# First product of a block inverse with 64 columns of the inverse as stationary operand, and the first loads of the recurrence on another queue

## Chip, cores, metric

The kernel runs on one core of a Trainium2 chip. The metric is device microseconds for one execution of the whole program. Engines are named as the profile names them: PE is TensorE (PEld its weight loads), DVE is VectorE, ACT is ScalarE, POOL is GpSimd, SP is SyncE, which here only issues DMAs; ACT can issue DMAs too (ACTq).

## What is computed

A one-layer encoder: layer norm, one input projection, a Fourier mixer and a bidirectional gated DeltaNet side by side, an output projection, layer norm, a squared-ReLU MLP, layer norm. 2048 tokens and 16 meta tokens, width 1024, 4 heads of 128. The part that matters is the DeltaNet in chunked form:

```
l_mat = einsum("rbhncd,rbhnsd->rbhncs", k_beta, k) * decay_strict
unit_lower = l_mat + eye(CHUNK)
rhs = concatenate([v_beta, k_beta * exp(g_cum)[..., None]], axis=-1)
sol = triangular_solve(unit_lower, rhs, left_side=True, lower=True, unit_diagonal=True)
...
def step(S, inp):
    v_new = val - kcd @ S
    o = qd @ S + attn @ v_new
    S = S * chunk_decay + kt.T @ v_new
```

The kernel works in chunks of 128 tokens (16 steps, two directions, 4 heads) and does not solve: it forms the inverse of the unit triangular 128x128 matrix of each head and multiplies by it.

## The kernel before

The program runs in stages: norm and Fourier transform, the q/k/v projection with its convolution, the projection of z and the gates (`phase_zg`, about 514 to 981 us), the recurrence (`phase_delta`, about 980 to 1233 us), merge and output projection, MLP. A scheduler lays out each engine's instructions; an engine then runs its own list in order.

**Side work.** While PE runs the projection of z and the gates (three f16 matmuls, L95 to L97, per product, PSUM tiles `mm`, added up by DVE at L652), `phase_zg` pops pieces from a generator, `Delta.prep`, two per pop. Each `yield` in that generator ends a piece. `prep` builds per chunk and direction the strictly triangular matrix `N` (L1095) and the attention matrix `A`, stores both to DRAM, cuts the 32x32 diagonal blocks out of `N` (`diag`, with a sign change on ACT, L1112), inverts these blocks on DVE (`invert_blocks`, L997/L999, tiles `ivq`, `ivt`), and lastly runs `solve` for step 0 of both directions.

**solve** puts the 128x128 inverse of one step and direction together from its four inverted 32x32 diagonal blocks, loaded as `ad`. `X` holds the inverse, `XT` its transpose; all these tiles carry the name `hb` in the profile, since they lie in the memory of former `hb` tiles. It is a chain of four products per head, each in f32, with `yield`s between:

- P1 (L1175, PSUM 128x64): stationary `N` (128 columns), moving 64 columns of `XT`; only two 32x32 blocks of the result are wanted. ACT copies them with a minus sign to `V` (L1177).
- P2 (L1181): stationary `V` (64 columns), moving 64 columns of `X`: the 32x32 blocks beside the diagonal. DVE transposes one into `XT` (L1182) and copies two into `X` (L1184).
- P3 (L1188): stationary 64 columns of `N`, moving `XT`; ACT copies it with a minus sign to `W` (L1189).
- P4 (L1193): stationary `W`, moving `X`: the 64x64 block, copied to `X` by DVE (L1194).

Before P1 the blocks `ad` are spread into `X` and `XT`, transposed by DVE (L1169) and as they are by ACT (L1170).

**step** (L1258 to L1303) is one step of the recurrence in one direction: `S` times k (L1258, then DVE makes `vt`, L1260), `S` times q (L1266, ACT makes `qs`, L1269), the inverse times `vt` (L1275, ACT makes `vn`, L1278), the state update (L1283, DVE L1289) and the output (L1295, DVE L1301). Its PSUM tiles are `psc`, those of `solve` `psh` in the recurrence and `psg` before it. In direction 1 the first step has no state, and its L1258, L1266 are absent.

**phase_delta** interleaves by hand, with `go`, the two directions' step s and the two `solve`s of step s+1. In step 0 the loads of `vt` and `ktk` were issued from ACT (`q = nc.scalar if step == 0`), as was that of `ad` for step 1; all other loads of the recurrence (`N`, `A`, `kq`: 256, 256 and 512 KB a step and direction; `vt`, `ktk`: 256 KB each; `ad`: 64 KB) go from SP, two steps ahead. ACT also issues the stores `gz` of the last groups of `phase_zg` (L930).

Of the kernel before, what the change touches and what calls it, by code (L numbers as in the profile page):

```python
# [18 lines left out]
P = 128  # L19
# [3 lines left out]
NT = 16  # L23
# [3 lines left out]
HD = 4  # L27
# [980 lines left out]
class Delta:  # L1008
    RING = 5

    def __init__(self, k, pr):
        self.k = k
        self.d1 = [k.dram.tile([P, 32, 32], F32, name="d1_%d" % b) for b in range(4)]
        self.d2 = [k.dram.tile([P, 32, 32], F32, name="d2_%d" % b) for b in range(4)]
        self.dm1 = k.dram.tile([HD, 16, 16], F32, name="dm1")
        self.dm2 = k.dram.tile([HD, 16, 16], F32, name="dm2")
        self.NAd = {(q, d): k.dram.tile([2, P, HD, P], F32, name="na_%d_%d" % (q, d))
                    for q in range(NT) for d in range(2)}
        self.o1 = {}
        self.N, self.A, self.kq = {}, {}, {}  # L1020

        t = [half_block(pr).rearrange("p a b c -> p (a b c)").bitcast(F32) for _ in range(4)]
        self.uq = [t[3][:, 1024 * d:1024 * d + 1024].rearrange("p (h e c) -> p h e c", h=HD, e=2) for d in range(2)]
        t = [u[:, 512 * j:512 * j + 512].rearrange("p (h c) -> p h c", h=HD) for u in t for j in range(4)]
        self.S = [k.kp.tile([P, HD, P], F32, name="Sm"), None]
        self.X = [t[0:2], t[2:4]]
        self.XT = t[4:6]
        self.V, self.W = [[u[:, :, 64 * d:64 * d + 64] for d in range(2)] for u in t[6:8]]
        self.Nf, self.Af = t[8:10], t[10:12]
        self.t = t  # L1030
        for t in self.X[0] + self.X[1] + self.XT + self.V + self.W:
            k.nc.gpsimd.memset(t, 0.0)
        self.nx = 0

    def open_prep(self, ctx):
        k, nc = self.k, self.k.nc
        self.sp = ctx.enter_context(k.pool("dsa"))
        self.pg = ctx.enter_context(k.pool("dpg", bufs=3, space=PSUM))
        self.mneg = self.sp.tile([P, 2, P], BF16, name="mneg")
# [37 lines left out]
    def stage2(self, n):  # L1077

        k, nc, sp = self.k, self.k.nc, self.sp
        E = []  # L1080
        kq = self.load_kq(n, sp, 2)
        for d in range(2):
            E.append((yield from self.decay(n + 1, d, P)))
        NA = [[sp.tile([P, HD, P], F32, name="%s%d" % (a, d), bufs=1) for a in "NA"] for d in range(2)]
        for j in range(2):
            yield
            ps = self.pg.tile([P, HD, P], F32, name="psg").rearrange("p (a b) c -> p a b c", b=2)
            for e in range(2):
                h = 2 * j + e
                nc.tensor.matmul(ps[:, e], lhsT=kq[:, h, 0], rhs=kq[:, h], start=True, stop=True)  # L1090
            hh = slice(2 * j, 2 * j + 2)
            for d in range(2):
                for e in range(2):
                    h = 2 * j + e
                    nc.vector.scalar_tensor_tensor(  # L1095
                        out=NA[d][0][:, h], in0=ps[:, e, 0], scalar=k.beta[:, n + 1, 4 * d + h:4 * d + h + 1],
                        in1=E[d][:, h], op0=ALU.mult, op1=ALU.mult)
                nc.vector.tensor_tensor(out=NA[d][1][:, hh], in0=ps[:, :, 1], in1=E[d][:, hh], op=ALU.mult)
        for d in range(2):
            st = self.chunk(n, d)  # L1100
            self.diag(NA[d][0], st, d)
            for a in range(2):
                nc.sync.dma_start(out=self.NAd[st, d][a], in_=NA[d][a])
        yield

    def diag(self, N, step, d):

        k, nc, sp = self.k, self.k.nc, self.sp
        nd = sp.tile([P, HD, 32], F32, name="nd", bufs=2)
        for b in range(4):  # L1110
            s = slice(32 * b, 32 * b + 32)
            nc.scalar.activation(out=nd[s], in_=N[s, :, s], func=AF.Copy, scale=-1.0)  # L1112
# [21 lines left out]
    def prep(self):  # L1134

        yield from self.stage2(0)
        yield from self.stage2(NT - 1)
        yield from self.meta()
        for half, bts in ((range(1, 4), (0, 3)), (range(4, 8), (1, 2))):
            for q in half:  # L1140
                yield from self.stage2(q)
                yield from self.stage2(NT - 1 - q)
            for b in bts:
                yield from invert_blocks(self.k, self.sp, self.d1[b], self.d2[b], 32, P)
                yield
        for d in range(2):
            self.N[0, d], self.A[0, d] = self.t[8 + d], self.t[10 + d]
            for a, u in enumerate((self.N, self.A)):
                self.k.nc.sync.dma_start(out=u[0, d], in_=self.NAd[0, d][a])
            self.kq[0, d] = self.uq[d]  # L1150
            self.k.nc.sync.dma_start(out=self.kq[0, d], in_=self.k.kqd[self.chunk(0, d)])
            yield
            yield from self.solve(0, d, self.sp, self.pg, "psg")

    def solve(self, step, d, sp, pp, pname):

        k, nc = self.k, self.k.nc
        N = self.N[step, d]
        ad = sp.tile([P, HD, 32], F32, name="ad", bufs=2)
        o = ((step % 4) * 2 + d) * 16  # L1160
        (nc.scalar if step == 1 else nc.sync).dma_start(out=ad, in_=self.d2[step // 4][o:o + 16].rearrange("(h b) r j -> (b r) h j", b=4))
        X, XT, V, W = self.X[d][step % 2], self.XT[d], self.V[d], self.W[d]
        blk = lambda b: slice(32 * b, 32 * b + 32)
        half = lambda a: slice(64 * a, 64 * a + 64)
        f, s = ((0, 1), (1, 0))[d]
        pair = lambda a, z: blk(2 * a + z)
        x, xt = (XT, X) if d == 0 else (X, XT)
        for b in range(4):
            nc.vector.transpose(xt[blk(b), :, blk(b)], ad[blk(b)])  # L1169
            nc.scalar.copy(x[blk(b), :, blk(b)], ad[blk(b)])  # L1170
        yield
        cols = lambda t, h, z: t[:, h].rearrange("p (a z c) -> p a z c", z=2, c=32)[:, :, z]
        ps = pp.tile([P, HD, P], F32, name=pname)
        for h in range(HD):
            nc.tensor.matmul(ps[:, h, :64], lhsT=N[:, h], rhs=cols(XT, h, f), start=True, stop=True)  # L1175
        for a in range(2):
            nc.scalar.activation(out=V[pair(a, s), :, blk(a)], in_=ps[pair(a, s), :, blk(a)], func=AF.Copy, scale=-1.0)  # L1177
        yield
        ps = pp.tile([P, HD, P], F32, name=pname)
        for h in range(HD):  # L1180
            nc.tensor.matmul(ps[:64, h, :64], lhsT=V[:, h], rhs=cols(X, h, s), start=True, stop=True)  # L1181
        nc.vector.transpose(XT[pair(f, s), :, pair(f, f)], ps[blk(f), :, blk(f)])  # L1182
        for a in range(2):
            nc.vector.tensor_copy(X[pair(a, f), :, pair(a, s)], ps[blk(a), :, blk(a)])  # L1184
        yield
        ps = pp.tile([P, HD, P], F32, name=pname)
        for h in range(HD):
            nc.tensor.matmul(ps[:64, h, :64], lhsT=N[:, h, half(s)], rhs=XT[:, h, half(f)], start=True, stop=True)  # L1188
        nc.scalar.activation(out=W[half(s)], in_=ps[:64, :, :64], func=AF.Copy, scale=-1.0)  # L1189
        yield  # L1190
        ps = pp.tile([P, HD, P], F32, name=pname)
        for h in range(HD):
# [44 lines left out]
    def step(self, step, d):  # L1237
# [99 lines left out]
def phase_delta(k, dl):  # L1337
    with ExitStack() as cd:
# [4 lines left out]
        def loads(upto):  # L1343
            while dl.loaded <= min(upto, NT - 1):
                for d in range(2):
                    dl.load(dl.loaded, d)
                dl.loaded += 1

        for s in range(NT):
            st = [dl.step(s, d) for d in range(2)]  # L1350
            if s == 0:
                for g in st:
                    next(g)
                loads(1)
            ho = [dl.solve(s + 1, d, dl.cp, dl.ph, "psh") for d in range(2)] if s < NT - 1 else [iter(())] * 2
            po, dl.posts = dl.posts, []
# [572 lines left out]
```

## Time and profile before

| what | us |
|---|---|
| median of 3 runs | 2716.14 |
| lowest and highest | 2711.14, 2718.16 |
| the profiled execution, its own time | 2715.62 |
| its span in the trace | 2713.8 |

The profiled execution lies 0.5 us under the median and 1.8 us over its own span, so a sum made on the trace can be set against the median within a microsecond. Times of the trace count from the span's start. A timeline row gives start, duration, engine, line, operation, tile read and written, shape, count, and in brackets the idle time before it with what ended it. PE shows two records for each f32 matmul, so x8 is one product of four heads; from the start of one row to that of the next is what the first one cost PE. The table of stretches gives for each engine its busy time and, after them, the granted clock of TensorE as a share of full speed, the busy share of the DMA engines and GB/s.

### The profile page before, as it was taken

To read this page: it belongs to the slowest core of one execution; us is meant where nothing else is said; L and a number is where in the kernel's file an instruction comes from. 1 tells how busy PE (TensorE), PEld (TensorE's weight loads), DVE (VectorE), ACT (ScalarE), POOL (GpSimd) and SP (SyncE) were. 2 spreads that over 40 slices of the span, in tenths; PEclk is the share of its full clock that TensorE was granted. 3 is DMA by queue.
4 is the path that set the end of the run, shared out by engine and by line. 5 is a ranking of instruction groups with operands and counts; after the bars stand their busy time and mean duration, and the time that the engine had idled before them with its cause. 6 is when DMAs were issued, how large, how long until landed. Compare 5 with 4: busy or idle time off the path is not lost.

```text
span 2713.8 us, 40453 instructions
## 1 busy us (share of the span) xinstructions
PE 2596.9 (96%) x14377; PEld 1371.4 (51%) x14377; DVE 1953.1 (72%) x3726; ACT 1206.4 (44%) x2752; POOL 402.3 (15%) x559
## 2 busy tenths in 40 slices
PE   7988999999999989999999999999999999999997
PEld 6455545444444469995444444444444444444443
DVE  7589897888976327798867788888888645554556
ACT  5454665655553335774222544444444432222232
POOL 1000231310100001462266300000002200000003
PEclk9999999999999989999999999999999999999999
DMA  7468475689889758767622864444447633333311
GB/s 264 157 215 297 167 252 168 197 285 309 295 313 296 246 186 252 245 192 232 203 94 92 237 251 142 153 140 144 150 167 278 218 109 101 101 101 102 103 41 74
DMA packets 321212, 513.29 MB, mean 189 GB/s; under 512 B 83697, under 2 KB 135873, under 8 KB 317041
## 3 DMA queue, kind: packets, MB, share of 16 engines
q1 hardware_dynamic: 317088, 506.30, 56.4%
q10 hardware_dynamic: 3920, 4.40, 0.5%
q8 instruction: 113, 1.85, 0.3%
q14 instruction: 91, 0.74, 0.1%
HBM read 307.10 MB, written 203.50 MB: 188 GB/s over the span
## 4 chain that ended last, share of the span: by engine, by line
PE 62%; DVE 16%; DMA 7%; ACT 4%; issue 4%; POOL 3%; SPq 1%; DVEq 0%; POOLq 0%; ACTq 0%
PE mm L95 17%; PE mm L97 16%; PE mm L96 16%; DVE wu L59 2%; DVE hb L59 1%; DVE hid L529 1%; PE psc L1258 1%; DVE conv L800 1%; DVE acc L1620 1%; PE psc L1295 1%; PE psc L1283 1%; PE psh L1175 1%; PE psc L1266 1%; POOL hr L1406 1%; PE psc L1275 1%
## 5 line engine op out<-in xcount | busy, mean ns | idle before, releaser
L95 PE MATMUL mm<-hb,wu 128*128 128x512 f16 x1280 | 487.5, 381 | 4.0 <-ACT ex L485 2.0
L96 PE MATMUL mm<-hb,wu 128*128 128x512 f16 x1280 | 487.7, 381 | 0.0
L97 PE MATMUL mm<-hb,wu 128*128 128x512 f16 x1280 | 487.4, 381 | 0.0
L1620 DVE TENSOR_TENSOR acc<-acc,mm 128x512 f32<-128x512 f32 x420 | 285.5, 683 | 149.4 <-PE mm L97 148.7
L95 PE MATMUL mm<-wdn,hid 128*128 128x512 f16 x904 | 342.6, 379 | 13.4 <-DVE acc L1620 13.3
L96 PE MATMUL mm<-wdn,hid 128*128 128x512 f16 x904 | 342.9, 380 | 0.0
L97 PE MATMUL mm<-wdn,hid 128*128 128x512 f16 x904 | 342.7, 380 | 0.2 <-DVE hid L529 0.2
L96 PEld LDWEIGHTS <-wu 128*128 128x128 f16 x1912 | 186.0, 98 | 226.1 <-issue 24.2
L97 PEld LDWEIGHTS <-wu 128*128 128x128 f16 x1912 | 185.8, 98 | 218.7 <-issue 8.8
L95 PEld LDWEIGHTS <-wu 128*128 128x128 f16 x1912 | 186.4, 98 | 213.5 <-issue 9.0
L95 PE MATMUL mm<-ht,wu 128*128 128x512 f16 x512 | 195.0, 381 | 4.8 <-DVE c L652 3.6
L529 DVE TENSOR_TENSOR hid<-c,hid 128x512 f16<-128x512 f32 x158 | 107.3, 686 | 124.9 <-ACT hid L528 124.6
L96 PE MATMUL mm<-ht,wu 128*128 128x512 f16 x512 | 194.8, 381 | 0.0
L97 PE MATMUL mm<-ht,wu 128*128 128x512 f16 x512 | 194.7, 380 | 0.0
L66 POOL TENSOR_SCALAR ln_rs<-ln_mv 128x1 f32<-128x1 f32 (+1 forms) x49 | 14.1, 287 | 1170.6 <-DVE ln_mv L76 1160.5
L528 ACT CAST hid<-c 128x512 f16<-128x512 f32 x158 | 95.7, 614 | 183.7 <-PE mm L97 155.1
L96 PEld LDWEIGHTS <-hid 128*128 128x128 f16 x904 | 88.4, 98 | 122.9 <-issue 20.0
L800 DVE SCALAR_TENSOR_TENSOR conv<-rawc,cw,conv 128x512 f32<-128x512 f32 x192 | 134.7, 741 | 15.7 <-ACT conv L798 15.2
L58 ACT ACTIVATE wdn<-raw 128x512 f16<-128x512 f32 x78 | 46.4, 622 | 222.7 <-PE mm L97 187.3
L97 PEld LDWEIGHTS <-hid 128*128 128x128 f16 x904 | 88.4, 98 | 108.5 <-DVE hid L529 2.2
L95 PEld LDWEIGHTS <-hid 128*128 128x128 f16 x904 | 88.4, 98 | 107.4 <-ACT hid L528 1.2
L58 ACT ACTIVATE wu<-raw 128x512 f16<-128x512 f32 x145 | 88.0, 622 | 73.8 <-PE mm L97 44.9
(384 smaller groups left out, 4957.4 us busy)
## 6 DMA issues: line engine op xcount, KB each, us to landing
wu<-op SPq DMA_DIRECT2D x245, 256.0 KB
op<-wu SPq DMA_DIRECT2D x203, 256.0 KB
wdn<-op SPq DMA_DIRECT2D x112, 256.0 KB
op<-wdn SPq DMA_DIRECT2D x98, 256.0 KB
kq<-kqd SPq DMA_DIRECT2D x46, 512.0 KB
raw<-in_w_down SPq DMA_DIRECT2D x36, 512.0 KB
raw<-in_w_qz SPq DMA_DIRECT2D x32, 512.0 KB
gt<-c SPq DMA_DIRECT2D x64, 256.0 KB
```

Of the source, the lines that this page charges most:

```text
L58: nc.scalar.activation(out=hi, in_=src, func=AF.Copy, scale=scale)
L59: nc.vector.scalar_tensor_tensor(out=lo, in0=src, scalar=scale, in1=hi, op0=ALU.mult, op1=ALU.subtract)
L95: mm(ps, lhsT=whi(q), rhs=xhi(q), start=first and q == 0, stop=False, skip_group_check=skip)
L96: mm(ps, lhsT=whi(q), rhs=xlo(q), start=False, stop=False, skip_group_check=skip)
L97: mm(ps, lhsT=wlo(q), rhs=xhi(q), start=False, stop=last and q == nk - 1, skip_group_check=skip)
L528: k.nc.scalar.copy(t[:, 0], src)
L529: k.nc.vector.tensor_tensor(out=t[:, 1], in0=src, in1=t[:, 0], op=ALU.subtract)
L800: nc.vector.scalar_tensor_tensor(out=s, in0=src[:, j:j + m], scalar=cw[:, c, j:j + 1], in1=s, op0=ALU.mult, op1=ALU.add)
L1175: nc.tensor.matmul(ps[:, h, :64], lhsT=N[:, h], rhs=cols(XT, h, f), start=True, stop=True)
L1258: nc.tensor.matmul(ps[:, h], lhsT=kq[:, h, 0], rhs=S[:, h], start=True, stop=True)
L1266: nc.tensor.matmul(psq[:, h], lhsT=kq[:, h, 1], rhs=S[:, h], start=True, stop=True)
L1620: nc.vector.tensor_tensor(out=c, in0=c, in1=ps, op=ALU.add)
```

## The change

`N` is stored negated (beta is negated once into `nbeta`), so no copy needs a minus sign. P1 changes its operands: stationary are 64 columns of `XT`, moving 64 columns of `N`, and the PSUM result has 64 partitions. It holds the wanted blocks transposed, so `V` is written by two DVE transposes (L1188 after) where ACT had two copies. The two copies after P2 go from DVE to ACT (L1195 after). So that the 64 columns of `XT` lie side by side, its column blocks are stored in another order (`col`), and P3 reads them with a stride. `solve` for step 0 inside `prep` yields twice where it yielded once. The loads of `vt`, `ktk` for step 0 and of `ad` for step 1 go from SP, ahead of the first `N`, `kq`, `A`.

```diff
-            yield from self.solve(0, d, self.sp, self.pg, "psg")
+            for _ in self.solve(0, d, self.sp, self.pg, "psg"):
+                yield
+                yield
...
+        col = lambda t, b: blk(b // 2 + b % 2 * 2) if t is XT else blk(b)
...
-            nc.tensor.matmul(ps[:, h, :64], lhsT=N[:, h], rhs=cols(XT, h, f), start=True, stop=True)
+            nc.tensor.matmul(ps[:64, h, :64], lhsT=XT[:, h, half(f)], rhs=cols(N, h, s), start=True, stop=True)
         for a in range(2):
-            nc.scalar.activation(out=V[pair(a, s), :, blk(a)], in_=ps[pair(a, s), :, blk(a)], func=AF.Copy, scale=-1.0)
+            nc.vector.transpose(V[pair(a, s), :, blk(a)], ps[blk(a), :, blk(a)])
...
         for a in range(2):
-            nc.vector.tensor_copy(X[pair(a, f), :, pair(a, s)], ps[blk(a), :, blk(a)])
+            nc.scalar.copy(X[pair(a, f), :, pair(a, s)], ps[blk(a), :, blk(a)])
...
-            nc.tensor.matmul(ps[:64, h, :64], lhsT=N[:, h, half(s)], rhs=XT[:, h, half(f)], start=True, stop=True)
-        nc.scalar.activation(out=W[half(s)], in_=ps[:64, :, :64], func=AF.Copy, scale=-1.0)
+            nc.tensor.matmul(ps[:64, h, :64], lhsT=N[:, h, half(s)],
+                             rhs=XT[:, h].rearrange("p (z a c) -> p a z c", z=2, a=2)[:, f], start=True, stop=True)
+        nc.scalar.copy(W[half(s)], ps[:64, :, :64])
...
-        q = nc.scalar if step == 0 else nc.sync
+        q = nc.sync
...
                 for g in st:
                     next(g)
+                for d in range(2):
+                    dl.ad[1, d] = dl.load_ad(1, d, dl.cp)
                 loads(1)
```

Three places in the engines' lists. First ACT's list at the entrance to the recurrence, before the change: behind the last gate store stand four loads of step 0 and the two `ad` loads of step 1.

```order
L929 ACTIVATE c2_10798<-c2_10798 128x512
L930 DMA gz_6516<-c2_10798 128x512
L1248 DMA vt_10960<-vtok_3172 128x512
L1251 DMA ktk_10962<-ktok_3171 128x512
L1248 DMA vt_10974<-vtok_3172 128x512
L1251 DMA ktk_10976<-ktok_3171 128x512
L1161 DMA ad_10991<-d2_0_6447 128x4x32
L1269 ACTIVATE qs_11018<-psc_11013,ex_3464 128x128 x4
L1161 DMA ad_11050<-d2_0_6447 128x4x32
```

And SP's list at the same place after the change: the same six loads stand behind the last weight load of `phase_zg` (`wu`) and ahead of `N`, `kq`, `A` of step 1, which stood directly behind `wu` before.

```order
L598 DMA wu_10690<-op_8800 128x1024
L1260 DMA vt_10962<-vtok_3172 128x512
L1263 DMA ktk_10964<-ktok_3171 128x512
L1260 DMA vt_10976<-vtok_3172 128x512
L1263 DMA ktk_10978<-ktok_3171 128x512
L1163 DMA ad_10981<-d2_0_6447 128x4x32
L1163 DMA ad_10983<-d2_0_6447 128x4x32
L1132 DMA N_10985<-na_1_0_6455 128x512
L1126 DMA kq_10987<-kqd_3165 128x1024
L1132 DMA A_10989<-na_1_0_6455 128x512
L1132 DMA N_10991<-na_1_1_6456 128x512
```

The loads of step 0 have left ACT's list, and the first `N` has moved back by six places of SP's.

Second PE's list in one step of the first half, before, from P1 of the second direction to P4: x4 is one product of four heads. P3 of the two directions (L1188) stand apart, with half a product of the next step between them.

```order
L1175 MATMUL psh_11997<-hb_6486,N_11746 128x64 x4
L1283 MATMUL psc_12004<-vn_11962,ktk_11892 128x128 x4
L1181 MATMUL psh_12014<-hb_6485,hb_6486 64x64 x4
L1283 MATMUL psc_12022<-vn_11982,ktk_11906 128x128 x4
L1295 MATMUL psc_12032<-vn_11962,A_11556 128x128 x4
L1181 MATMUL psh_12039<-hb_6485,hb_6486 64x64 x4
L1295 MATMUL psc_12047<-vn_11982,A_11562 128x128 x4
L1188 MATMUL psh_12054<-hb_6486,N_11740 64x64 x4
L1258 MATMUL psc_12083<-S0_12009,kq_11742 128x128 x2
L1188 MATMUL psh_12060<-hb_6486,N_11746 64x64 x4
L1193 MATMUL psh_12066<-hb_6485,hb_6486 64x64 x4
L1193 MATMUL psh_12072<-hb_6485,hb_6486 64x64 x4
```

After the change the same stretch reads so (L1186 is P1, L1192 P2, L1199 P3, L1205 P4; L1295 and L1307 are the state update and the output):

```order
L1186 MATMUL psh_11999<-N_11748,hb_6486 64x64 x4
L1295 MATMUL psc_12006<-vn_11964,ktk_11894 128x128 x4
L1192 MATMUL psh_12016<-hb_6485,hb_6486 64x64 x4
L1295 MATMUL psc_12024<-vn_11984,ktk_11908 128x128 x4
L1307 MATMUL psc_12034<-vn_11964,A_11558 128x128 x4
L1192 MATMUL psh_12041<-hb_6485,hb_6486 64x64 x4
L1307 MATMUL psc_12049<-vn_11984,A_11564 128x128 x4
L1199 MATMUL psh_12056<-hb_6486,N_11742 64x64 x4
L1199 MATMUL psh_12062<-hb_6486,N_11748 64x64 x4
L1270 MATMUL psc_12085<-S0_12011,kq_11744 128x128
L1205 MATMUL psh_12068<-hb_6485,hb_6486 64x64 x4
L1205 MATMUL psh_12074<-hb_6485,hb_6486 64x64 x4
```

P1 is 64x64, the two P3 stand together, and one head of the next step's L1270 stands between P3 and P4.

Third DVE's list in `phase_zg` where `solve` of step 0, direction 1, runs: before, the transpose after P2 (L1182) stands in the first third of the inversion of a group of blocks (L997, L999), among the additions to gate tiles (L652) and the splits of early weights (L59).

```order
L997 TENSOR_TENSOR ivt_9403<-ivq_9402 128x130
L59 SCALAR_TENSOR_TENSOR hb_9317<-raw_9732,hb_9317 128x512
L999 TENSOR_TENSOR ivq_9402<-ivq_9402,ivt_9403 128x26x5
L652 TENSOR_TENSOR c3_9534<-c3_9534,mm_9543 128x512
L997 TENSOR_TENSOR ivt_9403<-ivq_9402 128x150
L1182 STREAM_TRANSPOSE hb_6486<-psg_9718 32x4x32
L999 TENSOR_TENSOR ivq_9402<-ivq_9402,ivt_9403 128x25x6
L1184 COPY hb_6485<-psg_9718 32x4x32
L997 TENSOR_TENSOR ivt_9403<-ivq_9402 128x168
L1184 COPY hb_6485<-psg_9718 32x4x32
```

After the change that `solve` stands later in the inversion: its two transposes into `V` (L1188) and the one after P2 (L1193) are spread over it.

```order
L999 TENSOR_TENSOR ivq_9404<-ivq_9404,ivt_9405 128x19x12
L1188 STREAM_TRANSPOSE hb_6486<-psg_9821 32x4x32
L997 TENSOR_TENSOR ivt_9405<-ivq_9404 128x234
L1188 STREAM_TRANSPOSE hb_6486<-psg_9821 32x4x32
L999 TENSOR_TENSOR ivq_9404<-ivq_9404,ivt_9405 128x18x13
L926 SCALAR_TENSOR_TENSOR c2_9535<-c2_9535,yat_9541 128x512
L997 TENSOR_TENSOR ivt_9405<-ivq_9404 128x238
L999 TENSOR_TENSOR ivq_9404<-ivq_9404,ivt_9405 128x17x14
L997 TENSOR_TENSOR ivt_9405<-ivq_9404 128x240
L999 TENSOR_TENSOR ivq_9404<-ivq_9404,ivt_9405 128x16x15
L1193 STREAM_TRANSPOSE hb_6486<-psg_9844 32x4x32
L997 TENSOR_TENSOR ivt_9405<-ivq_9404 128x240
```

On PE, the f16 matmuls between two products of `solve` in `phase_zg` were 6, 18 and 6 in direction 0 and 24, 12 and 12 in direction 1, and 18 between the two directions; after the change they are 24 between any two, and 72 between the directions.

More of the change, by code (lines that the diff above doesn't have):

```diff
@@ L1018, in __init__ @@
                     for q in range(NT) for d in range(2)}
-        self.o1 = {}
+        self.o1, self.ad = {}, {}
         self.N, self.A, self.kq = {}, {}, {}
@@ L1038, in open_prep @@
         self.pg = ctx.enter_context(k.pool("dpg", bufs=3, space=PSUM))
+        k.nbeta = self.sp.tile([P, NT + 1, 8], F32, name="nbeta")
+        nc.vector.tensor_scalar(k.nbeta, k.beta, -1.0, None, op0=ALU.mult)
         self.mneg = self.sp.tile([P, 2, P], BF16, name="mneg")
@@ L1111, in diag @@
             s = slice(32 * b, 32 * b + 32)
-            nc.scalar.activation(out=nd[s], in_=N[s, :, s], func=AF.Copy, scale=-1.0)
+            nc.scalar.copy(nd[s], N[s, :, s])
             nc.gpsimd.memset(N[s, :, s], 0.0)
@@ L1152, in prep, with load_ad @@
             yield
-            yield from self.solve(0, d, self.sp, self.pg, "psg")
+            for _ in self.solve(0, d, self.sp, self.pg, "psg"):
+                yield
+                yield
+    def load_ad(self, step, d, sp):
+        ad = sp.tile([P, HD, 32], F32, name="ad", bufs=2)
+        o = ((step % 4) * 2 + d) * 16
+        self.k.nc.sync.dma_start(out=ad, in_=self.d2[step // 4][o:o + 16].rearrange("(h b) r j -> (b r) h j", b=4))
+        return ad
     def solve(self, step, d, sp, pp, pname):
@@ L1158, in solve @@
         N = self.N[step, d]
-        ad = sp.tile([P, HD, 32], F32, name="ad", bufs=2)
-        o = ((step % 4) * 2 + d) * 16
-        (nc.scalar if step == 1 else nc.sync).dma_start(out=ad, in_=self.d2[step // 4][o:o + 16].rearrange("(h b) r j -> (b r) h j", b=4))
+        ad = self.ad.pop((step, d)) if (step, d) in self.ad else self.load_ad(step, d, sp)
         X, XT, V, W = self.X[d][step % 2], self.XT[d], self.V[d], self.W[d]
```

6 lines of the change are left out of this document (3 added, 3 removed).

## Prediction

> **What bounds the kernel now.** The page first: PE is busy 96% of the span, and most of the chain that ended last is PE.
>
> ```profile
> PE 2596.9 (96%) x14377; PEld 1371.4 (51%) x14377; DVE 1953.1 (72%) x3726; ACT 1206.4 (44%) x2752; POOL 402.3 (15%) x559
> PE 62%; DVE 16%; DMA 7%; ACT 4%; issue 4%; POOL 3%; SPq 1%; DVEq 0%; POOLq 0%; ACTq 0%
> ```
>
> So time comes off where PE idles, runs at a low clock, or does less. The change touches the end of the side work in the gate projection (about 800 to 870 us) and the recurrence. The table of stretches, for the first, the entrance to the recurrence, one step of its first half and two of its second:
>
> ```profile
> 820.00:840.00 20.00, 16.66 (x86) 7.91 (x85) 18.40 (x49) 7.44 (x13) 0.16 (x1) 0.91 0.84 271
> 840.00:860.00 20.00, 20.00 (x95) 9.04 (x94) 18.34 (x45) 9.79 (x17) 0.00 (x0) 1.00 0.94 301
> 984.00:997.60 13.60, 8.47 (x38) 8.17 (x39) 4.41 (x16) 6.30 (x22) 2.08 (x2) 0.50 1.00 354
> 1082.90:1098.10 15.20, 15.14 (x146) 14.25 (x145) 10.66 (x35) 8.34 (x30) 2.08 (x2) 1.00 0.71 216
> 1159.70:1175.90 16.20, 16.10 (x154) 15.01 (x153) 15.34 (x40) 13.08 (x51) 11.71 (x15) 1.00 0.91 265
> 1192.20:1208.20 16.00, 16.00 (x153) 14.96 (x153) 15.51 (x41) 12.18 (x50) 10.82 (x15) 1.00 0.54 143
> ```
>
> Two stretches lose time: 820 to 840 (3.3 us idle, clock 0.91) and 984 to 997.6 (5.1 us idle, clock 0.50). The steps of the recurrence are full of PE work; in the second half DVE, with 15.3 to 15.5 us a step, is close behind.
>
> **Entrance to the recurrence.** The timeline of PE and ACT, and the chain there:
>
> ```profile
> 979.61 1.05 PE L1258 MATMUL psc<-Sm,hb 128*128 128x128 f32 x8
> 985.52 3.35 PE L1275 MATMUL psc<-vt,hb 128*128 128x128 f32 x14 [3.96 <-DVE vt L1260]
> 992.49 1.97 PE L1175 MATMUL psh<-hb,N 128*128 128x64 f32 x8 [3.61 <-ACT hb L1170]
> 1004.47 0.71 PE L1258 MATMUL psc<-S,kq 128*128 128x128 f32 x4
> 981.09 0.33 ACTq L930 DMA_DIRECT2D gz<-c  x1
> 981.46 3.56 DMA vt<-vtok
> 985.04 6.47 DMA ad<-d
> 985.52 0.63 ACT L1269 ACTIVATE qs<-psc,ex 128x128 f32<-128x128 f32 x2 [4.45 <-DMA ktk<-ktok]
> 995.08 1.14 ACT L1278 ACTIVATE vn<-psc,beta 128x128 f32<-128x128 f32 x4
> 996.10 1.20 ACT L1170 COPY hb<-ad 32x128 f32<-32x128 f32 x4
> 960.86 0.32 SPq L1130 DMA_DIRECT2D N<-na  x1
> 983.73 0.32 SPq L1130 DMA_DIRECT2D N<-na  x1
> ```
>
> ACT can issue `vt` only behind its last gate store at 981.09; PE waits 3.96 us for it, and 3.61 us more for `ad`, issued last. The clock is then halved until 997.6. From the first product of step 0 to that of step 1 it takes 1004.47 - 979.61 = 24.9 us. The work in it: 8 products of four heads with 128 columns, 2 P1 and 6 small products. With the costs shown next, 8 x 0.89 + 2 x 0.84 + 6 x 0.58 and some 0.4 for changes of shape, it is 12.7 us. So **12.2 us are lost**.
>
> After the change these six loads stand on SP behind the last `wu` load. SP was free there: in the trace its next issue, the first `N`, came at 960.86. The fourth came at 983.73, 2.6 us behind the gate store of 981.09: in the built program both queues' DMAs take turns on eight completion counters, and each waits for the one eight places ahead. Counting places, `vt` and `ktk` of direction 0 go at about 959 to 961, the last of the six behind a gate store near 977, and land before 981; `N` of direction 0 goes near 980, `kq` now waits for the store of 981.09, and `N` of direction 1 goes near 985. What is late next: ACT. From 981.4 it has 4 `qs` (1.2), 2 `vn` (0.6), then 4 copies of `ad` (1.2): P1 starts at about 984.4, where PE would come at 983.6 (0.8 lost). `N` of direction 1, at the 3.56 us of the `vt` load, is there by 988, where PE comes at 987.7 (0.3). I leave 1.2 us of waits and no half clock: **-11.0**. Bounds: 0, if the loads came no earlier, and -12.2. Behind those, `vt` of step 1 waits for the loads of steps 1 and 2 less the first `N`, 3.75 MB: at the 354 GB/s of 984 to 997.6 that is 10.6 us from 983.7, 994.3, when PE, earlier by then, is at 995: nothing, but with no margin.
>
> **Shape of P1.** PE in one step of the first half, and the end of a later one; the cost is start to start.
>
> ```profile
> 1069.17 1.06 PE L1266 MATMUL psc<-S,kq 128*128 128x128 f32 x8
> 1070.06 1.00 PE L1175 MATMUL psh<-hb,N 128*128 128x64 f32 x8
> 1070.90 1.11 PE L1275 MATMUL psc<-vt,hb 128*128 128x128 f32 x8
> 1071.85 1.06 PE L1266 MATMUL psc<-S,kq 128*128 128x128 f32 x8
> 1075.52 0.68 PE L1181 MATMUL psh<-hb 128*64 128x64 f32 x8
> 1076.12 1.16 PE L1283 MATMUL psc<-vn,ktk 128*128 128x128 f32 x8
> 1077.12 1.06 PE L1295 MATMUL psc<-vn,A 128*128 128x128 f32 x8
> 1078.11 0.68 PE L1181 MATMUL psh<-hb 128*64 128x64 f32 x8
> 1207.04 1.15 PE L1193 MATMUL psh<-hb 128*64 128x64 f32 x16
> 1208.11 2.05 PE L1258 MATMUL psc<-S,kq 128*128 128x128 f32 x16
> ```
>
> A wide product between wide ones costs 0.89 (1069.17 to 1070.06), P1 0.84, the wide one after P1 0.95. A small product costs 0.60, and 0.54 in a run of two (1.07 for x16); but the wide one after a small one costs 1.00, the one before it 0.99: each **change of width costs 0.10**. The new P1 has the small shape. One alone between wide ones takes 0.99 + 0.60 + 1.00 = 2.59 for 0.89 + 0.84 + 0.95 = 2.68: only 0.09 is won, where the rows of P1 and P2 alone suggest 0.24. Counted over the order of both programs (30 P1 in the recurrence): away go 30 x 0.84, 24 times 0.06 (0.95 - 0.89) in the wide product behind P1, and 6 times 0.10 where P2 stood behind it, 27.2; the small products grow from 41 single ones and 21 runs (49 products) to 56 and 30 (64), 0.60 and 0.54 each, +17.1; changes of width from 118 to 172, +5.4. Together **-4.7**. Bounds: -7.2 (30 x 0.24) and 0.
>
> The Trainium skill, "TensorE: Matmul & The Clock Gate", section "LDWEIGHTS (loading the stationary operand)", has a weight load take its number of columns over 1.2 GHz, so half the time for 64 columns. For 128 columns the trace agrees (107 ns by the page, 0.84 / 8 = 105 in P1); for 64 the page gives 53 ns, an estimate of 0.43 a product, where a single one shows 0.60, and that section has no price for a change of width. By that rule the term would be an estimated 30 x 0.41 = -12.3, by the rows it is -4.7.
>
> **Copies and transposes.** A wait of P4 in the first half, and groups of the tile:
>
> ```profile
> 1067.12 0.68 PE L1193 MATMUL psh<-hb 128*64 128x64 f32 x8 [0.35 <-ACT hb L1189]
> L1177 ACT ACTIVATE hb<-psh x60: 250/268/271, 994.5 to 1217.3; 32x128 f32<-32x128 f32 x60
> L1184 DVE COPY hb<-psh x60: 278/284/288, 999.0 to 1220.9; 32x128 f32<-32x128 f32 x60
> L1182 DVE STREAM_TRANSPOSE hb<-psh x30: 305/308/313, 998.7 to 1220.3; 32x128 f32<-32x128 f32 x30
> ```
>
> A `solve` takes 2 x 308 - 2 x 284 = 48 ns more of DVE; ACT gives 2 x 268 and takes two copies of the same blocks, of which no row stands on ACT without a scale: 268 by L1177, the nearest, with L1170's 0.30 as the other end. That is 0.1 us of DVE a step: in the first half DVE has 4.5 us to spare, in the second 0.5 to 0.9 us, and a shorter step takes most of that. `V` now comes through DVE's queue, but P2 stands behind P1 by one to three wide products (1 to 3 us), which covers 0.6 us of transposes. The state update L1289 stands behind `V` of direction 1 on DVE; it needs a product that PE makes after that P1, so it waits for nothing new. P4 of direction 1 waits 0.35 us for `W` in the row above; P3 of both directions now stand together, which brings that `W` 0.4 us earlier. I take -0.5 for all waits in the steps, bounds +2.5 (12 steps of 0.2, DVE late) and -3. Negating beta is one DVE instruction beside PE work: 0.
>
> **Side work.** The rows in the gate projection:
>
> ```profile
> 820.15 0.68 PE L1181 MATMUL psg<-hb 128*64 128x64 f32 x8
> 825.57 0.68 PE L1188 MATMUL psg<-hb 128*64 128x64 f32 x8 [3.34 <-DVE hb L1182]
> 825.20 0.31 DVE L1182 STREAM_TRANSPOSE hb<-psg 32x128 f32<-32x128 f32 x1
> 826.84 0.52 PE L95 MATMUL mm<-hb,wu 128*128 128x512 f16 x1
> 830.02 0.55 PE L97 MATMUL mm<-ht,wu 128*128 128x512 f16 x1
> PE mm L95 <- DVE c L652: 3.6, 3, 1.8
> ```
>
> P3 of direction 1 came 12 f16 matmuls behind P2, and its transpose 4.4 us late in DVE's queue: PE idled 3.34 us, then ran the matmuls from 826.84 to 830.4 at half clock. With a clock of 0.91 over 20 us, all of its loss in busy time, that is 1.7 us. After, 24 matmuls at 0.21 us (x95 in the 20 us from 840 to 860), 5.1 us, lie between any two products: more than the 4.4. So **-5.0**. Bounds: -5.1, and +1.8: DVE now stands before `V` of direction 1 until PE reaches its P1, some 8 us by my count, and the inversion and splits behind it move into 860 to 880; a wait of PE for an addition stuck there is the L652 row, 1.8 at most.
>
> **Sum.** -11.0 - 4.7 - 0.5 - 5.0 = -21.2 on 2715.6 of the profiled execution (0.5 under the median): **2694.4**.
>
> **Rivals.**
> - *Side work gives nothing*: DVE's wait for P1 brings back what the spacing wins. For: DVE is 92% busy from 820 to 860. Against: after 860 its stretch empties. 2699.4.
> - *The entrance gives half*: at the 216 GB/s of a step in the first half the 3.75 MB take 17.4 us; `vt` of step 1 comes at 1001.1, 6 us behind PE, and a half clock as from 826.84 to 830.4 adds 1.7: 2702. For: the loads of two steps stand ahead of it. Against: the DMA engines moved 354 GB/s when they had a queue.
> - *The new P1 doesn't shorten PE at all*: its changes of width eat it. 2699. Against: 0.09 a product by the rows.
> - *The cost goes by the stationary columns alone*: P1's 0.84 halves to 0.42, and changes of width are free; the term is 30 x 0.42 = -12.6: 2686.5. For: P1's weight loads set its pace. Against: the 0.60 of a small product. This is the section's rule named above.
> - *Slower*: DVE becomes the bound. `V` in its queue holds the state update L1289 behind it; S is what the next step begins with. If that comes w late in each of 15 steps, the gain is gone at w = 21.2/15 = 1.4 us, and from 1.9 the kernel is slower by over 0.3%. At w = 2: 2725. Against: 0.6 us of transposes is all that stands there.
>
> **How the numbers follow.** Forecast 0.62 (2690 to 2700), side work 0.12, entrance half 0.13, P1 no shorter 0.04, cost by columns 0.05, slower 0.04. The range 2685 to 2706 holds the forecast with the bounds of its terms and the cases but the slow one. Under 0.3% (8.1 us), about what a measurement of this kernel tells from no change, needs two terms to fail at once: 0.07. Faster 0.89, slower 0.04.
>
> **What would show it.** Entrance: no row of PE with a wait for `vt` or `ad` above 1 us, clock 1.0 from 980 on, 12 us from the first to the second step's first product. Steps: 14.6 to 14.9 us in the first half, P1 0.60 alone, wide neighbours at 0.99. Side work: no wait of PE for DVE at P2 or P3, clock 1.00. Wrong if `vt` of step 1 is waited for, or if steps of the second half stay at 16 us with DVE full.

## Result, and the profile after

The changed kernel took 2698.61 us (median of 4 runs, 2697.33 to 2702.70), the kernel before 2713.65 on the same chip (4 runs): a ratio of 0.9937, 95% interval 0.9922 to 0.9953, or -17 us (-13 to -21); the two medians are 15.0 us apart. That lies inside the range, 4 us above the forecast. The profiled execution of the changed kernel has a span of 2697.4 us, 16.4 under the one of before. Where the 16.4 came from, by the starts of the same products in both traces:

| stretch | before | after | difference |
|---|---|---|---|
| start to the first product of step 0 | 979.61 | 977.41 | -2.2 |
| steps 0 to 3 | 70.08 | 62.61 | -7.5 |
| steps 4 to 14 | 174.46 | 169.58 | -4.9 |
| step 15 to the end of PE | 1474.41 | 1472.52 | -1.9 |

The first and the last row of this table lie within what executions differ by: a second execution of the changed kernel has 979.32 for the first, and the kernel with the yields alone (below), which behind step 0 is the kernel before, 1471.10 for the last. The page's rows of busy time and of the chain, as quoted of before:

```profile
PE 2583.1 (96%) x14377; PEld 1358.3 (50%) x14377; DVE 1955.2 (72%) x3727; ACT 1202.4 (45%) x2752; POOL 403.4 (15%) x559
PE 60%; DVE 18%; DMA 8%; issue 4%; POOL 4%; ACT 3%; SPq 1%; DVEq 0%; POOLq 0%; ACTq 0%
```

PE is 13.8 us less busy, with the same number of matmuls; DVE and DMA have more of the chain.

**Entrance, after.** The timeline of PE and two pieces of the chain there (start, duration, engine, what):

```profile
977.41 1.05 PE L1270 MATMUL psc<-Sm,hb 128*128 128x128 f32 x8
981.86 0.68 PE L1186 MATMUL psh<-N,hb 128*64 128x64 f32 x8 [0.24 <-ACT hb L1181]
987.26 0.65 PE L1186 MATMUL psh<-N,hb 128*64 128x64 f32 x8 [1.57 <-DMA N<-na]
990.70 0.49 PE L1270 MATMUL psc<-S,kq 128*128 128x128 f32 x2
997.65 0.49 PE L1287 MATMUL psc<-vt,hb 128*128 128x128 f32 x2 [2.74 <-DVE vt L1272]
984.25 5.24 DMA kq<-kqd
989.51 7.65 DMA vt<-vtok
```

Step 0 went from 24.86 to 13.29 us: `vt` and `ad` of the first steps are not waited for, except 0.24 us for the spreading of `ad`. But step 1 went from 11.31 to 16.19: its `vt` could go only at 989.51, when an earlier `kq` had landed, and took 7.65 us more, so PE waited 2.74 us. A stretch at half clock follows. The table of stretches (columns as before: busy time of PE, PEld, DVE, ACT and POOL, clock, DMA share, GB/s):

```profile
820.00:840.00 20.00, 17.64 (x102) 8.54 (x101) 19.08 (x50) 7.62 (x15) 0.00 (x0) 1.00 0.90 314
984.00:997.65 13.65, 9.32 (x99) 8.41 (x98) 3.64 (x11) 4.91 (x15) 0.00 (x0) 1.00 1.00 354
997.65:1001.10 3.45, 3.45 (x18) 3.45 (x19) 2.95 (x11) 0.79 (x4) 2.08 (x2) 0.56 1.04 406
1084.08:1098.76 14.68, 14.68 (x146) 13.55 (x144) 10.80 (x34) 8.15 (x31) 2.10 (x3) 1.00 0.73 225
```

The first row is for the side work, below. The DMA engines are full from 984 to 997.65 us (share 1.00). The clock of 0.56 over 3.45 us costs 1.5 us. The last row is one step of the first half: 14.68 us where it was 15.14, full of PE work at full clock.

**P1, after.** PE in a step of the first half:

```profile
1072.55 1.06 PE L1278 MATMUL psc<-S,kq 128*128 128x128 f32 x8
1073.54 0.68 PE L1186 MATMUL psh<-N,hb 128*64 128x64 f32 x8
1074.14 1.16 PE L1287 MATMUL psc<-vt,hb 128*128 128x128 f32 x8
1075.14 1.06 PE L1278 MATMUL psc<-S,kq 128*128 128x128 f32 x8
1083.00 1.15 PE L1199 MATMUL psh<-hb,N 128*64 128x64 f32 x16
1084.08 0.38 PE L1270 MATMUL psc<-S,kq 128*128 128x128 f32 x1
1084.49 1.15 PE L1205 MATMUL psh<-hb 128*64 128x64 f32 x16
1085.57 1.83 PE L1270 MATMUL psc<-S,kq 128*128 128x128 f32 x14
```

Start to start, P1 costs 0.60 (1073.54 to 1074.14), the wide product before it 0.99, the one after it 1.00, and two small ones together 1.08 (1083.00 to 1084.08), as the prediction had it.

The two P4 also take 1.08 now (1084.49 to 1085.57). Before, they took 1.30 in the same place of a step, for the second waited some 0.2 us for `W`, too short to be listed as a wait. Two rows of before show it; the row after them is the sum of all listed waits of P4 for `W` in the recurrence (us in total, times, longest), and the last one is the same sum after the change:

```profile
1081.57 1.37 PE L1193 MATMUL psh<-hb 128*64 128x64 f32 x16
1082.87 1.60 PE L1258 MATMUL psc<-S,kq 128*128 128x128 f32 x12
PE psh L1193 <- ACT hb L1189: 0.4, 1, 0.4
PE psh L1205 <- ACT hb L1201: 1.1, 3, 0.5
```

So the wait went from the full steps of the first half and is longer in others.

**Side work, after.** PE, DVE and SP in the gate projection, then the same two instructions, SP's load of `raw` and DVE's L624, in the kernel before:

```profile
826.55 0.68 PE L1186 MATMUL psg<-hb 128*64 128x64 f32 x8
831.21 0.30 DVE L1188 STREAM_TRANSPOSE hb<-psg 32x128 f32<-32x128 f32 x1
832.28 0.65 PE L1192 MATMUL psg<-hb 128*64 128x64 f32 x8 [2.36 <-DVE hb L1188]
856.95 0.32 SPq L1000 DMA_DIRECT2D d<-ivq  x1
859.30 0.49 SPq L615 DMA_DIRECT2D raw<-in_w_down  x1
865.95 0.69 DVE L624 TENSOR_TENSOR sum<-raw,sum 128x512 f32<-128x512 f32 x1 [5.08 <-DMA raw<-in_w_down]
867.29 0.38 PE L95 MATMUL mm<-ht,wu 128*128 128x512 f16 x1 [1.75 <-DVE c L652]
```

```profile
848.25 0.47 SPq L615 DMA_DIRECT2D raw<-in_w_down  x1
855.50 0.68 DVE L624 TENSOR_TENSOR sum<-raw,sum 128x512 f32<-128x512 f32 x1
861.68 0.32 SPq L1000 DMA_DIRECT2D d<-ivq  x1
```

The wait of 3.34 us at P3 has become one of 2.36 at P2. DVE comes to the transposes 4.0 us after that P1 ends, and between P1 and P2 stand 12 f16 matmuls (827.16 to 829.7), not 24. And something new is late: a weight load `raw` for a later stage stood ahead of the store of the block inverses (L1000) in SP's list, and now stands behind it. It goes 11 us later, DVE waits 5.08 us for it in front of an addition (L652), and PE 1.75 us behind that. (In the kernel before, PE waited 0.6 us for ACT in the same place.)

### The profile page after: what moved, and what is told of

Read it like the earlier page. It is cut to its first block, busy times and chain, and to the rows that moved or that the text cites. A ratio compares the mean times of both kernels' runs of the same rounds, so it can differ in the third digit from the quotient of the medians.

```text
span 2697.4 us, 40475 instructions
## 1 busy us (share of the span) xinstructions
PE 2583.1 (96%) x14377; PEld 1358.3 (50%) x14377; DVE 1955.2 (72%) x3727; ACT 1202.4 (45%) x2752; POOL 403.4 (15%) x559
## 4 chain that ended last, share of the span: by engine, by line
PE 60%; DVE 18%; DMA 8%; issue 4%; POOL 4%; ACT 3%; SPq 1%; DVEq 0%; POOLq 0%; ACTq 0%
PE mm L95 16%; PE mm L97 16%; PE mm L96 16%; DVE wu L59 2%; DVE hb L59 1%; PE psc L1270 1%; DVE hid L529 1%; PE psc L1287 1%; PE psc L1295 1%; PE psc L1278 1%; DMA raw<-in_w_down 1%; DVE conv L800 1%; DVE acc L1634 1%; POOL hr L1420 1%; PE psc L1307 1%
## 5 line engine op out<-in xcount | busy, mean ns | idle before, releaser
L66 POOL TENSOR_SCALAR ln_rs<-ln_mv 128x1 f32<-128x1 f32 (+1 forms) x49 | 14.1, 287 | 1169.9 <-DVE ln_mv L76 1159.7
```

## Experiments

Changes in us are the ratio's distance from 1 times the median of before in the same batch, with the interval of 95%.

### One part at a time

The loads alone:

```diff
-        (nc.scalar if step == 1 else nc.sync).dma_start(out=ad, in_=...)
+        ad = self.ad.pop((step, d)) if (step, d) in self.ad else self.load_ad(step, d, sp)
...
-        q = nc.scalar if step == 0 else nc.sync
+        q = nc.sync
...
+                for d in range(2):
+                    dl.ad[1, d] = dl.load_ad(1, d, dl.cp)
```

> Before, with nothing changed but the six first loads: `vt` and `ktk` of step 0 and `ad` of step 1 go from SP ahead of the first `N`. Theory A (the entrance gives half, since `vt` of step 1 comes late behind 4 MB of `N`, `kq`, `A`): -4 to -7 us against before, with no wait of PE for `vt` or `ad` in step 0, a wait of 2 to 4 us for `vt` in step 1, and a stretch at half clock behind it. Theory B (the step of the prediction): -10 to -12 us, and no wait for `vt` of step 1. Theory C (the loads alone do nothing, the gain of the changed kernel in this place needs the shorter P1): within 1.5 us of before.

Measured: ratio 0.9972 (0.9962 to 0.9983), -7.6 us (-10.3 to -4.6). PE of that kernel, from the first product of step 0 to that of step 1:

```profile
983.53 1.05 PE L1263 MATMUL psc<-Sm,hb 128*128 128x128 f32 x8
993.74 1.08 PE L1180 MATMUL psh<-hb,N 128*128 128x64 f32 x8 [1.21 <-DMA N<-na]
999.02 1.16 PE L1263 MATMUL psc<-S,kq 128*128 128x128 f32 x8
```

Step 0 is 9.4 us shorter (15.49), steps 1 to 3 together 1.3 longer: 8.1 in all. That is between theories A and B, nearer to A by size; but the wait for `vt` of step 1 was only 0.43 us and no half clock followed, so A's mechanism is not what held it here. Part of what held it is the wait of 1.21 us for `N` in the rows above. Theory C is out.

The yields alone:

```diff
-            yield from self.solve(0, d, self.sp, self.pg, "psg")
+            for _ in self.solve(0, d, self.sp, self.pg, "psg"):
+                yield
+                yield
```

> Before, with nothing changed but two yields for one in `solve` of step 0 inside the gate projection. Theory A (the yields put 12 f16 matmuls, 2.6 us, between any two products, and DVE's queue there is 4 us long): PE still waits 1.5 to 2.5 us for DVE at P3 of direction 1, no half clock; -1 to -3 us. Theory B (the step of the prediction): no wait, -5 us. Theory C (what is won at P3 is lost to additions that come later): within 1 us.

Measured: ratio 1.0000 (0.9990 to 1.0009), 0 us (-2.7 to +2.4). PE and DVE of that kernel:

```profile
839.27 1.01 PE L1190 MATMUL psg<-hb 128*64 128x64 f32 x7 [2.42 <-DVE hb L1184]
870.76 0.69 DVE L624 TENSOR_TENSOR sum<-raw,sum 128x512 f32<-128x512 f32 x1 [5.44 <-DMA raw<-in_w_down]
872.11 0.38 PE L95 MATMUL mm<-ht,wu 128*128 128x512 f16 x1 [1.38 <-DVE c L652]
```

The wait of A is there (2.42 us), but with half a clock behind it, which A did not expect: seven of the eight matmuls of that product take 1.01 us where all eight took 0.68. So little was won at this place against the 3.34 us and half clock of before, and PE waits 1.38 us behind the late `raw`, which is C's mechanism. Theory B is out.

The new P1 alone, with all that belongs to it: the changed kernel with the two diffs above undone.

> Before, with the new P1 and all that belongs to it (`N` negated, `V` by DVE transposes, copies after P2 on ACT, the other order of columns in `XT`), but the loads of step 0 and `ad` of step 1 still from ACT and one yield in the side work. Theory A (0.09 us a product by widths, with the waits in the steps): -4 to -6 us, a step of the first half 0.4 to 0.6 us shorter. Theory B (the cost goes by stationary columns alone, 53 ns for 64 of them): -11 to -13 us, 0.8 us a step. Theory C (DVE pays for it; what PE saves is lost to waits): within 2 us. In the gate projection V now waits in DVE's queue too, which may cost up to 2 us in each theory.

Measured: ratio 0.9968 (0.9957 to 0.9980), -8.7 us (-11.7 to -5.4). In the traces the recurrence accounts for 6.2 of it (steps 0 to 3: 67.49 for 70.08; steps 4 to 14: 170.83 for 174.46), a step of the first half for 0.45 (14.69 for 15.14). Theory C is out, and so is B in the first half, where a step is 0.45 shorter and not 0.8. The size is above A's; the interval reaches down to 5.4. The copies that moved between ACT and DVE were not measured apart from the shape of P1.

The three parts alone add up to -16.3 us, and all together gave -17: within the intervals, each some 3 us to either side, no part is seen to depend on another.

### The yields taken out of the changed kernel, and doubled again

> The changed kernel with its doubled yields undone. Theory A (the yields are worth nothing: what PE no longer waits at P3 it waits later for additions, since DVE then waits 5 us for a weight load `raw` that stands behind the store of the block inverses in SP's list): within 1.5 us of the changed kernel, -13 to -18 against before; L624 of DVE does not wait for `raw` in this kernel, as it does in the changed one, and a wait at P2 is there instead. Theory B (the step of the prediction, 12 f16 matmuls between products): 3 to 5 us slower than the changed kernel, -9 to -12 against before.

Measured: ratio 0.9938 (0.9926 to 0.9951), -16.8 us, as fast as the changed kernel. SP and DVE of that kernel:

```profile
849.41 0.42 SPq L615 DMA_DIRECT2D raw<-in_w_down  x1
862.30 0.32 SPq L1000 DMA_DIRECT2D d<-ivq  x1
856.68 0.69 DVE L624 TENSOR_TENSOR sum<-raw,sum 128x512 f32<-128x512 f32 x1
```

`raw` is back ahead of L1000, and L624 waits for nothing; waits of 2.01 us at P2 of direction 0 and 1.65 at P3 of direction 1 are there instead. Theory A holds in its size, and in what it says of `raw`. That is the same in all 13 profiles: with one yield (five kernels) L624 never waits for `raw`, with two or four (eight profiles) it always does, 4.2 to 6.5 us. What it costs PE differs: behind it PE waited 1.4 to 3.1 us for an addition in four of the eight, less than 1 us or not at all in three, and in the one with four yields 1.32 us for ACT; with one yield PE waited 0.6 to 1.9 us for ACT in the same place in four of five. So the late `raw` is shown, and how much of the gain it took is not.

Four yields for one:

```diff
             for _ in self.solve(0, d, self.sp, self.pg, "psg"):
                 yield
                 yield
+                yield
+                yield
```

> The changed kernel with four yields for one in `solve` of step 0, so that 24 f16 matmuls (5.2 us) or more stand between most of its products where 12 stand in the changed kernel. Theory A (the 12 matmuls are too few for DVE's queue, which answers P1 after 4.3 us): the 2.4 us wait at P2 goes, and the kernel is 2 to 4 us faster than the changed one (about -18 to -20 against before). Theory B (DVE has more work than time in that place; what PE doesn't wait at P2 it waits for additions at L652 or later): within 1.5 us of the changed kernel.

Measured: ratio 0.9941 (0.9926 to 0.9955); the changed kernel, run once more in the same batch, had 0.9948 (0.9932 to 0.9964). No product of `solve` waits in the side work any more, and the kernel is no faster by more than the intervals: theory B by its size. From the last product of `stage2` to the first of step 0, PE took 211.1 us before and 209.8 to 213.1 in all twelve other profiles, whatever the yields.

### The changed kernel again

> The changed kernel again, as it is, for a direct comparison with the runs of its own batch: -13 to -19 us against before. The wait for `vt` of step 1 (2.7 us) and that at P2 in the gate projection (2.4 us) are seen again if they belong to the kernel, and not if they belong to one execution.

Measured: -14.1 us (-18.5 to -9.8). The wait at P2 was there (1.91 us), the one for `vt` of step 1 only with 0.36 and no half clock behind it; steps 0 to 3 took 59.96 us where the first profile had 62.61. So some 2.6 us of the stretch at 997 belong to one execution. But steps 4 to 14 took 172.13 us where the first profile had 169.58: one profile tells the time of a stretch to within some 2.5 us. Behind the late `raw` PE waited 2.77 us here, with half a clock behind it.

### The order of the first loads

`N`, `kq`, `A` of step 2 behind `vt`, `ktk` of step 1:

```diff
                 go(st[1], po[1])
+            if s == 1:
+                loads(2)
             go(ho[0])
-            loads(s + 2)
+            if s > 0:
+                loads(s + 2)
```

> The changed kernel, with `N`, `kq`, `A` of step 2 loaded behind `vt` and `ktk` of step 1 instead of ahead of them. Theory A (`vt` of step 1 is late because 2 MB of step 2 stand ahead of it): the 2.7 us wait for it and the half clock behind it go, -4 to -5.5 us against the changed kernel (about -19 to -21 against before). Theory B (the DMA engines are full from 984 to 1000 us whatever the order; the wait moves to `N` or `kq` of step 2): within 1.5 us of the changed kernel.

Measured: ratio 0.9937 (0.9925 to 0.9949), the same as the changed kernel. PE of that kernel in step 2:

```profile
1006.81 0.65 PE L1186 MATMUL psh<-N,hb 128*64 128x64 f32 x8 [0.49 <-PE psc L1278]
1007.29 0.63 PE L1192 MATMUL psh<-hb 128*64 128x64 f32 x8
1008.56 0.65 PE L1192 MATMUL psh<-hb 128*64 128x64 f32 x8 [0.64 <-DVE hb L1188]
1010.12 0.68 PE L1199 MATMUL psh<-hb,N 128*64 128x64 f32 x8 [0.91 <-DVE hb L1193]
```

The wait for `vt` went, and step 1 took 10.66 us. But the scheduler now laid the products of the next `solve` with nothing between them, so they wait for DVE's transposes, and the granted clock was 0.78 from 1006.8 to 1014.4; step 2 took 21.42 where the changed kernel has 16.44. The gain is given back, by another way than theory B had.

Both `N` of step 1 ahead of its `kq` and `A`:

```diff
-                loads(1)
+                dl.load_split(1)
+                dl.loaded = 2
```

(`load_split` issues `N`, `N`, `kq`, `kq`, `A`, `A`.)

> The changed kernel with the loads of step 1 in the order `N`, `N`, `kq`, `kq`, `A`, `A` instead of `N`, `kq`, `A` twice. Theory A (the wait of 1.6 us at P1 of direction 1 is a term by itself): that wait goes, -1.5 us against the changed kernel. Theory B (the bytes ahead of `vt` of step 1 set the time at which step 1 can go on, whatever stands before): the wait at P1 goes or shrinks and the wait for `vt` of step 1, 2.7 us, grows by as much; within 0.7 us of the changed kernel.

Measured: ratio 0.9944 (0.9931 to 0.9958), the same as the changed kernel in its batch. The wait at P1 of direction 1 stayed (1.74 us), since that product had also moved up by 2.4 us (984.84), and a stretch of half clock came behind it, so step 0 took 16.50 us; no wait for `vt` of step 1 is seen. Neither theory's mechanism; the size is B's. In every order tried, steps 0 to 3 take 59 to 63 us, while the prediction's costs give some 54 for the products in them. What would take the rest away was not found.

### Fewer changes of width

P1 of both directions together, and P2 of both:

```diff
             go(st[0])
-            go(ho[0])
             go(st[0])
             go(st[1], st[1])
-            go(ho[1], ho[1])
-            go(st[0])
-            go(ho[0])
-            go(st[1])
-            go(st[0])
-            go(ho[1])
-            go(st[1])
+            go(ho[1])
+            go(ho[0], ho[1])
+            go(st[0])
+            go(st[1])
+            go(ho[0], ho[1])
+            go(st[0])
+            go(st[1])
```

> The changed kernel with the hand-written order altered so that P1 of both directions stand together, and P2 of both too. Theory A (a change of width costs 0.10 us; two single small products cost 2 x (0.60 + 0.20), a pair 1.07 + 0.20, so 0.33 less, two pairs a step): a step of the first half about 14.0 us instead of 14.69, -6 to -10 us against the changed kernel (about -22 to -26 against before). Theory B (no cost of width; P2 so close behind P1 waits for DVE's transposes of V): a row of PE with a wait for DVE at P2 or P3 in most steps, and 0 to +8 us against the changed kernel.

Measured: ratio 0.9921 (0.9907 to 0.9935), -21 us, 7 less than the changed kernel in the same batch. A step of the first half took 14.27 us, for P4 was still in two pieces.

All four in pairs (the edit against the kernel with two pairs):

```diff
             go(ho[0], ho[1])
             go(st[0])
-            go(st[1])
             go(po[0])
-            go(ho[0])
-            go(ho[1])
+            go(ho[0], ho[1])
+            go(st[1])
             go(po[1])
-            go(ho[0])
-            go(ho[1])
+            go(ho[0], ho[1])
```

> The changed kernel with all four products of `solve` in pairs: P1 of both directions, two state updates, P2 of both, one output, P3 of both, the other output, P4 of both. Theory A (each change of width 0.10 us, a pair 1.07): 10 wide products at 0.89 and 4 pairs at 1.27 make a step of the first half of 14.0 us where the changed kernel takes 14.69; -8 to -11 us against the changed kernel (about -23 to -27 against before). Theory B (P3 stands 0.9 us behind P2 and waits for DVE's transpose and ACT's copies): waits of 0.3 us or more at P3 or P4 in most steps, and the step stays at 14.3 us or above.

Measured: ratio 0.9911 (0.9898 to 0.9925), -24 us (-28 to -20): the fastest version here, 7.3 less than the changed kernel with single yields in the same batch. PE of that kernel, one step of the first half, then a row of its waits in the recurrence (us in total, times, longest):

```profile
1068.53 1.15 PE L1186 MATMUL psh<-N,hb 128*64 128x64 f32 x16
1069.60 2.05 PE L1295 MATMUL psc<-vn,ktk 128*128 128x128 f32 x16
1071.58 1.15 PE L1192 MATMUL psh<-hb 128*64 128x64 f32 x16
1072.66 1.60 PE L1307 MATMUL psc<-vn,A 128*128 128x128 f32 x12
1074.19 1.15 PE L1199 MATMUL psh<-hb,N 128*64 128x64 f32 x16
1075.27 0.71 PE L1307 MATMUL psc<-vn,A 128*128 128x128 f32 x4
1075.91 1.18 PE L1205 MATMUL psh<-hb 128*64 128x64 f32 x16
1077.02 2.05 PE L1270 MATMUL psc<-S,kq 128*128 128x128 f32 x16
PE psc L1287 <- DVE vt L1272: 3.8, 4, 1.9
```

A pair costs 1.07 to 1.11, and the step 14.05 us, where 10 x 0.89 + 4 x 1.27 = 13.98 was expected: theory A. The total came out a little under A's 8 to 11. PE now waits for DVE at L1287, 3.8 us in all and 3.0 of them in the second half, where DVE was busy for 14.40 of the 14.90 us from 1134.9 to 1149.8; that may be why, but the interval would also hold A's size.

> The kernel with all four products in pairs and the doubled yields undone. If the yields are worth nothing here too, within 1.5 us of the kernel with pairs alone; if they are worth the 5 us of the prediction, that much slower.

Measured: ratio 0.9913 (0.9898 to 0.9928), within 0.6 us of the kernel with pairs and doubled yields. The yields are worth nothing here either, as far as the intervals show.

## Why the prediction was right in its total, and where it was wrong

| term | predicted | measured alone |
|---|---|---|
| entrance (loads) | -11.0 | -7.6 (-10.3 to -4.6) |
| shape of P1, and waits in the steps | -4.7 - 0.5 = -5.2 | -8.7 (-11.7 to -5.4) |
| side work (yields) | -5.0 | 0.0 (-2.7 to +2.4) |
| sum | -21.2 | -16.3; all together -17 |

**Side work: wrong.** The step that failed is "24 matmuls at 0.21 us ..., 5.1 us, lie between any two products: more than the 4.4". The trace after has 12 matmuls between any two products, 2.6 us, and 36 between the directions; the trace before has 3, 9 and 3 in direction 0 and 12, 6 and 6 in direction 1. That is half of each count: the built order lists a weight load and a matmul for each, and its rows were taken for matmuls. With 24 real ones the wait does go, and even that gains nothing that the intervals show. The step also left out the loads on SP's list that the moved pieces pass: `raw` fell behind L1000, DVE waited 5 us for it, and in the first profile 1.75 us of that came back to PE through L652. The rival "side work gives nothing" is right in its number and not in its mechanism: it had DVE standing before `V` until PE reached P1, but no wait of DVE for P1 is seen in the first profile; PE waited for DVE (2.36 us), and DVE for `raw`. How the lost 5 us divide between the two is not settled.

**Entrance: right mechanism, too large by 3.4.** `vt` and `ad` of the first steps vanished as waits, and step 0 of the first profile became 11.6 us shorter. What fell short is "nothing, but with no margin" for `vt` of step 1. The rate was right, 354 GB/s from 984 to 997.65, and so was the time at which PE came there (997.65 - 2.74 = 994.9, for 995). The bytes were not: 354 GB/s from 984 until DVE had that `vt` (997.25) make 4.7 MB, not 3.75. The sum left out the 0.25 MB of that `vt` itself, and loads issued behind it, such as `ktk` and the other `vt`, were in the engines too. A wait for `vt` of step 1 is also what the prediction named as a sign of being wrong. The rival "the entrance gives half" described the first profile (2.74 us of wait and a half clock), though its 216 GB/s did not; in the second run of the same kernel the wait was 0.36. In the kernel with the loads alone that wait was 0.43, and the shortfall lies elsewhere: step 0 took 15.49 us, where 24.9 - 11.0 = 13.9 was expected, and steps 1 to 3 were 1.3 longer. The wait for `N` of direction 1 was 1.57 for an expected 0.3, and that for ACT 0.24 for 0.8.

**Shape of P1: right.** 0.60 alone, 0.99 and 1.00 beside it, 14.69 a step (14.6 to 14.9 expected). The two kernels in pairs tested the cost of a change of width, and the step of 13.98 worked out from it came out at 14.05. The Trainium skill, "TensorE: Matmul & The Clock Gate", section "LDWEIGHTS (loading the stationary operand)", would give an estimated -12.3 for this term; the trace does not agree for a product that stands alone, 0.60 where that rule gives 0.43, and the new P1 alone measured -8.7 with an interval that ends at -11.7. Inside a run the trace is near that rule: eight more matmuls take 0.47 us (1.15 for x16 less 0.68 for x8). What it has no price for is the cost at the two ends of a run.

**Waits in the steps: not settled.** The prediction named the wait of P4 for `W`. It went from the full steps of the first half, some 0.2 us a step, since P3 of both directions now stand in one pair; in other steps it grew (1.1 us listed for 0.4). Of the 6.2 us by which the new P1 alone shortens the recurrence, 4.7 are the shape by the prediction's sum. The 1.5 that are left are less than the 2.5 by which two executions of the changed kernel differ in steps 4 to 14, so no run shows that the waits won more than the 0.5. In the second half, steps 10 to 14 took 15.90 us on average for 16.11 before, so little was won there.

**Luck in the total.** The side work and the loads fell short by 5.0 and 3.4 us, and the new P1 measured 3.5 more than was forecast for it, for reasons that the runs do not settle. That the total came so close is in part luck.

**The slower rival** is out: no state update of DVE was waited for in steps 1 to 15 of the changed kernel, and DVE took 10.80 of 14.68 us in a step of the first half.

## What to carry over

Where products of two shapes alternate on PE, count the changes of shape and cost each one from the trace: putting equal shapes side by side was worth about as much here (7 us) as the new operands themselves (8.7). When side work is spread further, follow what its pieces push back on the queue that issues the loads, for the wait that goes may come back through a load that is now late. A list of loads moved earlier has to be followed to the next load behind it; with the DMA engines full, count all bytes in flight and not only those ahead.

## What was not expected of the hardware

Waits of PE of 2 to 3 us were followed by half a clock in some places and not in others. In the first profile of the changed kernel the wait of 2.74 us was (0.56 over the 3.45 us behind it), the one of 2.36 us at P2 was not (granted clock 1.00 from 820 to 840). The length of the wait does not decide it: one of 2.06 us at P2 in the kernel with the new P1 alone was, and one of 2.89 us at P2 in the kernel with both `N` first was not. The stretches behind these two, from the table of stretches:

```profile
814.80:818.20 3.40, 3.40 (x14) 1.45 (x13) 0.31 (x1) 0.51 (x2) 0.00 (x0) 0.50 1.01 324
831.11:840.00 8.89, 8.89 (x56) 4.57 (x57) 8.48 (x21) 1.84 (x5) 0.00 (x0) 1.00 0.93 353
```

So a wait of this length costs either its own length or some 1.7 us more (half of 3.4), and one profile does not say which. What decides it is not shown.
